# A run-time test moved ahead of the last expert place, and the last layer's x summed in PSUM

## The chip, the cores and the metric

The kernel runs on one core of a Trainium2 chip. The metric is the device time of one execution in microseconds (us); the times below are medians of several executions. The engines are TensorE (PE in the profile, its weight loads PEld), VectorE (DVE), ScalarE (ACT), GpSimd (POOL) and SyncE (SP), which issues most transfers.

## What is computed

Two layers of a trunk work on 256 tokens of x and 256 tokens of a context, each 1024 wide. A layer norms and modulates its input, mixes tokens in three branches (gated linear attention, Fourier, windowed attention), adds the result to x, and then runs a mixture of 16 experts in four groups with two experts for each token. Layer 1, the last, keeps x alone. At the end x is normed once more.

```python
x = x + gate1[:, None, :] * y
h2 = modulate(rms_norm(x, g_ffn), shift2, scale2)
x = x + gate2[:, None, :] * hierarchical_moe(h2, ...)      # out += (silu(h @ w1[e]) * (h @ w3[e])) @ w2[e] * gates[:, e]
...
return rms_norm(x, g_final)                                # after layer 1
```

## The kernel before

The expert stage (`moe`) handles the 16 experts as 16 places, ordered by how many tokens they have. A place is big (B, up to 128 tokens, split in high and low fp32r halves) or small (s, up to 64 tokens, plain fp32). In layer 0 the places are `BBBBsBBsBBsBBsss`, in layer 1 `BBBsssBssssBssss`; the last two are small in both. For a small place PE multiplies the gathered tokens by w1 and w3 (`pair`, L1646, 32 passes in two halves: the first by `begin` in the place before), ACT and DVE make the gated hidden values `th` (L1697, L1658 to L1660), PE transposes them (L1665), and PE multiplies by w2 (L1646, out `c`). The places up to 13 scatter their result rows to a table `yb` in DRAM (L1564). Places 14 and 15 do not: their result is scaled by the gate `gsl`, split in a high and a low half (L1733, L1734), kept in SBUF in a ring slot (`last_y`), and put back to token rows by a product with a one-hot matrix `oh` (`put_rows`, L1776).

Weights come in pieces of 1 MB, each in a ring slot (`wraw`), issued by SP (L245) in the order of `pieces_of` as slots become free. Four slots, `self.spare`, leave the ring before the end. Before the change two of them took the results of places 14 and 15, and two the rows of `yb` (`rows`, L1760), which POOL adds up (L1761); PE then adds them by a product with the identity (L1779) in the same PSUM sum as the one-hot products. DVE multiplies the sum by the modulation `gb` (L1797) and adds it to x (L1799). In layer 0 four row tiles are handled, t = 0 and 1 of x and t = 2 and 3 of the context, which come later; in layer 1 there are two.

If an expert has more tokens than its place can hold, a general path (`moe_general`) adds what is left directly to x. Whether it runs is known only at run time: every engine reads a count `cnti` (L1784, `values_load`) and branches over the block (L1785, `tc.If`). With these inputs the block is not entered. The framework orders instructions by the program's order, the dependences and a planner's estimate of when they are ready; an If is placed as one block. Behind the block, on the path that skips it, each engine waits for its own older work and sets its semaphores as if the block had run; for SP this is its DMA queues. Before the change the block had a pool of its own (`gen`), and stood in the program behind place 15 and the one-hot products of place 14.

At the end (`finish`) ACT squares x from SBUF (L423), POOL takes the power -1/2 (L415), DVE multiplies by the factor and `g_final` (`gf`, L1864), and SP writes 128 rows (L1865). L1912 is the end of the program.

## Time and profile before

| what | us |
|---|---|
| median of 3 runs (lowest, highest) | 1570.74 (1569.88, 1577.3) |
| the profiled execution | 1564.04 |
| its span from the first to the last instruction | 1562.3 |
| mean granted TensorE clock, share of full | 0.975 |

The page lists busy time by engine, the span in slices, the transfers, the chain of work that ended last and the costliest groups of instructions. All times of rows are in us from the start of the span unless marked ns. A row of a timeline merges equal instructions in a stretch; the name before the arrow is what is written, and the brackets hold the idle time of the engine before it and what ended that time. An engine name with q stands for the engine's queue processor: semaphores, branches, register loads and transfer issues.

### The profile page before, as it was taken

How to read it: one execution, taken by the hardware profiler on the slowest of the kernel's cores; microseconds unless marked ns; L12 is line 12 of the kernel's file. 1: busy time of each engine (PE TensorE's matmuls, PEld its weight loads, DVE VectorE, ACT ScalarE, POOL GpSimd, SP SyncE). 2: the span in 40 equal slices, each digit the busy share in tenths (PEclk: the TensorE clock that was granted, in tenths of full speed). 3: DMA queues.
4: the chain of work that ended last, by engine and by line, in shares of the span. 5: the costliest groups of instructions: out<-in, count | busy, mean ns of one | idle time of the engine just before them, and what ended most of it. 6: DMA issues, size and time to landing. Idle time of an engine off the chain costs nothing. (4 is left out here: it accounts for less than half of the span.)

```text
span 1562.3 us, 22623 instructions
## 1 busy us (share of the span) xinstructions
PE 1437.5 (92%) x8333; PEld 1029.9 (66%) x8333; DVE 937.5 (60%) x1757; ACT 746.8 (48%) x1286; POOL 214.0 (14%) x238
## 2 busy tenths in 40 slices
PE   6999899999999998899999979999899979998885
PEld 4666666677777798676665428687689967553521
DVE  4379767432366786897776327467965689341412
ACT  4568556422223232576665306668654448341411
POOL 1124100000111101111111014023001111021001
PEclk9999999999999998999999988999999989999998
DMA  9772242543556578799999863322335699999992
GB/s 325 205 222 92 95 152 68 182 134 122 175 188 203 189 226 317 248 348 379 394 378 385 303 242 118 130 84 82 98 109 185 216 339 334 378 386 394 395 360 120
DMA packets 230795, 363.17 MB, mean 232 GB/s; under 512 B 25676, under 2 KB 125206, under 8 KB 230676
## 3 DMA queue, kind: packets, MB, share of 16 engines
q1 hardware_dynamic: 223808, 349.77, 64.2%
q0 software_dynamic: 6432, 11.76, 2.1%
q8 instruction: 69, 1.13, 0.3%
q14 instruction: 50, 0.41, 0.1%
q10 hardware_dynamic: 436, 0.10, 0.0%
HBM read 350.56 MB, written 21.82 MB: 238 GB/s over the span
## 5 line engine op out<-in xcount | busy, mean ns | idle before, releaser
L266 DVE TENSOR_TENSOR wlo<-wraw,whi 128x1024 fp32r<-128x1024 f32 (+1 forms) x324 | 377.9, 1180 | 184.8 <-ACT whi L265 126.7
L265 ACT ACTIVATE whi<-wraw 128x1024 fp32r<-128x1024 f32 (+1 forms) x324 | 322.3, 1010 | 258.6 <-PE pa L229 110.4
L228 PE MATMUL pa<-hhi,whi 128*128 128x512 f32 (+1 forms) x704 | 240.0, 356 | 1.9 <-ACT qT L795 1.0
L229 PE MATMUL pa<-hlo,whi 128*128 128x512 f32 (+1 forms) x704 | 237.7, 352 | 0.0
L228 PEld LDWEIGHTS pa<-hhi,whi 128*128 128x128 f32 x704 | 133.3, 189 | 27.9 <-issue 10.0
L231 PE MATMUL pa<-hhi,wlo 128*128 128x512 f32 (+1 forms) x704 | 150.5, 349 | 0.0
L1646 PE MATMUL pa<-wraw,xh 128*64 128x512 f32 x520 | 147.2, 626 | 0.0
L229 PEld LDWEIGHTS pa<-hlo,whi 128*128 128x128 f32 x704 | 133.4, 190 | 19.4 <-issue 6.5
L231 PEld LDWEIGHTS pa<-hhi,wlo 128*128 128x128 f32 x704 | 113.5, 190 | 19.2 <-issue 4.8
L1659 DVE SCALAR_TENSOR_TENSOR th<-th,pa 64x512 f32<-64x512 f32 (+1 forms) x32 | 21.7, 679 | 122.6 <-ACT th L1658 122.5
L770 POOL TENSOR_TENSOR m<-m,gu 128x512 f32<-128x512 f32 (+1 forms) x32 | 37.5, 1171 | 403.9 <-DVE gu L768 403.9
L1646 PEld LDWEIGHTS pa<-wraw,xh 128*64 128x64 f32 x520 | 43.7, 142 | 74.4 <-issue 71.3
L235 PE MATMUL pa<-whi,xh 128*128 128x512 f32 x208 | 84.9, 408 | 3.8 <-ACT whi L265 3.7
L236 PE MATMUL pa<-wlo,xh 128*128 128x512 f32 x208 | 85.8, 413 | 1.5 <-DVE wlo L266 1.4
L237 PE MATMUL pa<-whi,xl 128*128 128x512 f32 x208 | 83.6, 402 | 0.1
L1646 PE MATMUL c<-wraw,hh 128*64 128x512 f32 x256 | 69.3, 631 | 1.0 <-DVE hh L1702 1.0
L236 PE MATMUL pa<-y,whi 128*128 128x512 f32 (+1 forms) x192 | 66.3, 345 | 0.9 <-DVE y L272 0.9
L1558 POOL DMA_INDIRECT xg<-h2b,tki x30 | 33.4, 1113 | 242.6 <-PE c L1630 75.1
L235 PE MATMUL pa<-y,whi 128*128 128x512 f32 (+1 forms) x192 | 65.4, 341 | 0.7 <-DVE mx L1150 0.7
L237 PE MATMUL pa<-y,wlo 128*128 128x512 f32 (+1 forms) x192 | 64.9, 338 | 0.0
L359 DVE SCALAR_TENSOR_TENSOR adaw<-adaw,cT 128x512 f32<-128x512 f32 x56 | 45.3, 809 | 25.1 <-DMA adaw<-in_w_ada_dram 24.4
L1564 POOL DMA_INDIRECT yb<-ye,yki x28 | 28.4, 1013 | 220.0 <-ACT ye L1728 111.5
(456 smaller groups left out, 2792.0 us busy)
## 6 DMA issues: line engine op xcount, KB each, us to landing
wraw<-in_w_dram SPq DMA_DIRECT2D x184, 1024.0 KB
wraw<-in_w_in_dram SPq DMA_DIRECT2D x44, 1024.0 KB
adaw<-in_w_ada_dram SPq DMA_DIRECT2D x80, 512.0 KB
adaw<-in_w_ada_dram SPq DMA_DIRECT2D x8, 1024.0 KB
wraw<-in_w_out_dram SPq DMA_DIRECT2D x8, 1024.0 KB
x<-in_w_dram SPq DMA_DIRECT2D x8, 1024.0 KB
yb<-zero SPq DMA_DIRECT2D x12, 512.0 KB
wraw<-yb SPq DMA_DIRECT2D x6, 1024.0 KB
```

The source lines that it names most:

```text
L228: mm(out, lh, rh, start=(i == 0), stop=False)
L229: mm(out, lh, rl, start=False, stop=False)
L231: self.mm = mm(out, ll, rh, start=False, stop=(i == len(ops) - 1))
L235: mm(out, lh, rh, start=start, stop=False)
L236: mm(out, lh, rl, start=False, stop=False)
L237: self.mm = mm(out, ll, rh, start=False, stop=stop)
L265: self.sp = nc.scalar.activation(hv[:, :, q], v[:, :, q], AF.Copy)
L266: self.sl = self.lo.tensor_sub(lv[:, :, q], v[:, :, q], hv[:, :, q].bitcast(F32))
L359: nc.vector.scalar_tensor_tensor(v[:, j], v[:, j], ck, acc, op0=OP.mult, op1=OP.add)
L770: nc.gpsimd.tensor_add(self.m[:, j, :], self.m[:, j, :], u[:, :TY])
L1558: return nc.gpsimd.indirect_dma_start(out=xgs[e % len(xgs)][:n], out_offset=None, in_=h2b, in_offset=bass.IndirectOffsetOnAxis(ap=tki[:n, ...
L1646: nc.tensor.matmul(ps[ts(i, SM)], xs[:, k0[0] + k, :], w[:, k, :], start=(k0[0] + k == 0), stop=(k0[0] + k == k0[1] - 1))
```

## The change

The general path's test is moved from behind place 15 to the start of place 15 (in both layers). Ahead of it all weight pieces that are left are requested in order (`self.got.update(self.pieces)`). The general path has no pool of its own any more: it works in two of the four spare slots (`own`), with smaller weight blocks (512 rows by 128 columns instead of 1024 by 128 or 512 by 256), so it has more and smaller products. The row tiles t = 0 and 1 of `yb` are then loaded in these same two slots.

In layer 1 the results of places 14 and 15 are multiplied by the gate and by the modulation (`gbs`, loaded twice on 64 partitions in place 14) in one DVE operation before they are split. The rows of `yb` are multiplied by `gb` and added to x on DVE, x is added in PSUM by a product with the identity, and then come the one-hot products of place 15. So the new x stands whole in PSUM (`self.last_x`); x in SBUF is not completed. `finish` squares and scales it from PSUM in halves of 512 columns. In layer 0 the sums are made as before, behind the test.

```diff
         for e in range(NE):
+            if e == NE - 1:
+                self.got.update(self.pieces)
+                own = [self.spare.pop(0).tile([P, 2048], F32, name="wraw") for _ in range(2)]
+                n = nc.values_load(cnti[0:1, 0:1], min_val=0, max_val=T)
+                with tc.If(n > 0):
+                    self.moe_general(l, T, h2b, gun, gund, gb, own)
...
                 gb = self.mod_bcast(rp, l, 3, ns, "gb")
+                if l:
+                    gbs = rp.tile([P, 512], F32, name="gbs")
+                    for o in range(2):
+                        nc.sync.dma_start(gbs[ts(o, SM)], self.modd[l][3, 0, ts(o, 512)].partition_broadcast(SM))
...
                 ye = last_y(e)[:, :, :512]
+                if l:
+                    yg = rp.tile([P, 512], F32, name="yg")
+                    V.scalar_tensor_tensor(yg, p2, gsl[:, e:e + 1], gbs, op0=OP.mult, op1=OP.mult)
+                    self.evict_hl(ye[:, 0], ye[:, 1], yg)
+                    continue
...
-            yr = (self.spare.pop(0) if t < 2 else rq).tile([P, 2048], F32, name="wraw").rearrange("p (r d) -> p r d", r=2)
+            yr = own.pop(0) if t < 2 else rq.tile([P, 2048], F32, name="wraw")
+            yr = yr.rearrange("p (r d) -> p r d", r=2)
...
-                if 1 in js:
+                if 1 in js and not l:
                     i = nc.tensor.matmul(pt[o], self.ident, yrs[t][:, 0, ts(o, 512)], start=False, stop=True)
...
-        n = nc.values_load(cnti[0:1, 0:1], min_val=0, max_val=T)
-        with tc.If(n > 0):
-            self.moe_general(l, T, h2b, gun, gund, gb)
+        if l:
+            assert not any(big[NE - 2:])
+            for t in range(nt):
+                yr = yrs[t][:, 0]
+                V.tensor_mul(yr, yr, gb[:, 0])
+                V.tensor_add(self.x[:, t], self.x[:, t], yr)
+                for o in range(2):
+                    nc.tensor.matmul(pts[t][o], self.ident, self.x[:, t, ts(o, 512)], start=False, stop=False)
+            for t in range(nt):
+                put_rows(t, pts[t], (1,))
+            self.last_x = pts
+            sr.close()
+            self.sd.close()
+            return
...
     def finish(self, out):
         for t in range(2):
-            with self.soon(t + 1):
-                r = self.row_rstd(tp, t)
-                o = tp.tile([P, D], F32, name="o", bufs=2)
-                nc.vector.scalar_tensor_tensor(o, self.x[:, t, :], r, gf, op0=OP.mult, op1=OP.mult)
-                nc.sync.dma_start(out[0, ts(t, P), :], o)
+            r = tp.tile([P, 2], F32, name="r", bufs=2)
+            ss = tp.tile([P, 2], F32, name="ss", bufs=2)
+            jk = tp.tile([P, D], BF, name="jk", bufs=2)
+            for h in range(2):
+                nc.scalar.activation(jk[:, ts(h, 512)], self.last_x[t][h], AF.Square, accum_out=ss[:, h:h + 1])
+            nc.vector.tensor_scalar(r[:, 0:1], ss[:, 0:1], 1.0 / D, EPS, op0=OP.mult, op1=OP.add)
+            nc.vector.scalar_tensor_tensor(r[:, 1:2], ss[:, 1:2], 1.0 / D, r[:, 0:1], op0=OP.mult, op1=OP.add)
+            nc.gpsimd.tensor_tensor(r[:, 1:2], r[:, 1:2], self.nhalf[:, 0:1], op=OP.pow)
+            o = tp.tile([P, D], F32, name="o", bufs=2)
+            for h in range(2):
+                nc.vector.scalar_tensor_tensor(o[:, ts(h, 512)], self.last_x[t][h], r[:, 1:2], gf[:, ts(h, 512)],
+                                               op0=OP.mult, op1=OP.mult)
+            nc.sync.dma_start(out[0, ts(t, P), :], o)
```

## Rows read from the trace of the kernel before

**Rows 1.** Page, part 1: busy time, share of the span, instructions of each engine.
```profile
PE 1437.5 (92%) x8333; PEld 1029.9 (66%) x8333; DVE 937.5 (60%) x1757; ACT 746.8 (48%) x1286; POOL 214.0 (14%) x238
```

**Rows 2.** Chain that ended last, in order of time: start, us, what.
```profile
1546.42 3.16 PE pa L1779 x4
...
1553.05 1.44 POOL rsr L415
...
1556.55 1.28 DVE o L1864
```

**Rows 3.** Instructions of line L1785: min/median/max ns, first and last start; below, who waited.
```profile
L1785 SPq EVENT_SEMAPHORE  x16: 17/17/17, 914.8 to 1532.7; - x16
...
L1785 DVEq COMPARE_BRANCH  x2: 63/68/72, 933.3 to 1542.0; - x2
L1785 PEldq COMPARE_BRANCH  x2: 3420/3432/3445, 934.0 to 1542.0; - x2
L1785 DVEq EVENT_SEMAPHORE  x2: 21/21/21, 936.1 to 1542.5; - x2
...
  DVE x L1799: 2.9, 1
```

**Rows 4.** Windows: length, busy (count) of PE, PEld, DVE, ACT, POOL; PE clock, DMA share, GB/s.
```profile
934.40:937.60 3.20, 0.01 (x1) 0.00 (x0) 1.40 (x2) 0.14 (x1) 0.00 (x0) 1.00 0.03 8
937.60:941.20 3.60, 3.50 (x9) 2.30 (x9) 2.14 (x5) 2.16 (x4) 1.39 (x3) 0.54 0.02 5
941.20:946.20 5.00, 3.46 (x16) 3.04 (x16) 2.62 (x1) 1.34 (x3) 5.00 (x3) 0.50 0.00 0
...
1537.00:1541.00 4.00, 3.65 (x16) 1.06 (x16) 0.09 (x1) 0.15 (x1) 0.00 (x0) 1.00 0.00 0
...
1545.60:1549.00 3.40, 3.38 (x6) 1.48 (x6) 0.54 (x1) 0.00 (x0) 0.00 (x0) 0.52 0.02 6
```

**Rows 5.** Timeline, end of layer 1: start, us, engine, line, operation, count, idle before.
```profile
1519.16 0.43 PE L1665 MATMUL c<-ident,th 64*128 64x64 f32 x4 [2.86 <-DVE th L1660]
...
1526.64 0.69 ACT L1733 ACTIVATE wraw<-c,gsl 128x512 fp32r<-128x512 f32 x1 [9.05 <-PE c L1646]
...
1529.70 3.65 PE L1646 MATMUL pa<-wraw,xh 128*64 128x512 f32 x14
...
1540.85 0.69 ACT L1733 ACTIVATE wraw<-c,gsl 128x512 fp32r<-128x512 f32 x1 [6.22 <-PE c L1646]
1541.57 0.75 DVE L1734 SCALAR_TENSOR_TENSOR wraw<-c,gsl,wraw 128x512 fp32r<-128x512 f32 x1 [4.48 <-ACT wraw L1733]
...
1545.62 0.79 PE L1776 MATMUL pa<-wraw,oh 64*128 64x512 f32 x2 [3.30 <-PEq L1785]
...
1554.09 1.06 ACT L423 ACTIVATE jk<-x 128x1024 bf16<-128x1024 f32 x1 [1.35 <-DVE x L1799]
...
1555.05 0.19 ACT L423 ACTIVATION_READ_ACCUMULATOR jk<-x 128x1 f32 x1
...
1555.96 0.56 POOL L415 TENSOR_TENSOR rsr<-rsr,nhalf 128x1 f32<-128x1 f32 x1 [1.46 <-DVE rsr L414]
```

**Rows 6.** Timeline, end of the expert stage of layer 0.
```profile
911.39 0.69 ACT L1733 ACTIVATE wraw<-c,gsl 128x512 fp32r<-128x512 f32 x1 [12.09 <-PE c L1646]
...
913.58 3.65 PE L1646 MATMUL pa<-wraw,xh 128*64 128x512 f32 x14
...
932.63 0.69 DVE L1797 TENSOR_TENSOR wraw<-c,gb 128x512 f32<-128x512 f32 x1 [0.17 <-PE c L1779]
936.21 2.36 DVE L1799 TENSOR_TENSOR x<-x,wraw 128x1024 f32<-128x1024 f32 x2 [2.89 <-DVEq L1785]
```

**Rows 7.** Timeline, the row loads on SP and POOL's additions.
```profile
1519.70 0.88 SPq L1760 DMA_DIRECT2D wraw<-yb  x2
...
1530.47 4.73 POOL L1761 TENSOR_TENSOR wraw<-wraw 128x1024 f32<-128x1024 f32 x2 [15.63 <-DMA wraw<-yb]
```

**Rows 8.** SP's own waits in layer 0, 898 to 925: us in total, times, longest.
```profile
SPq L245 <- DMA wraw<-in_w_in_dram: 4.1, 1, 4.1
```

More of the change, by code (lines that the diff above doesn't have):

```diff
@@ L1666, in hidden @@
             return pt[:, :4 * n]
-        yes = []
+        yes, own = [], []
         def last_y(e):
@@ L1775, in put_rows @@
                             lh, rh = oh[ts(o, SM), j, ts(t, P)], yes[j][ts(o, SM), u, :512]
-                        nc.tensor.matmul(pt[o], lh, rh, start=(j + u == 0), stop=False)
+                        nc.tensor.matmul(pt[o], lh, rh, start=(j + u == 0), stop=(l + j + u == 3))
             for o in range(2):
-                if 1 in js:
+                if 1 in js and not l:
                     i = nc.tensor.matmul(pt[o], self.ident, yrs[t][:, 0, ts(o, 512)], start=False, stop=True)
@@ L1803, in moe, with moe_general @@
         self.dump(f"x2{l}", self.x[:, :nt])
-    def moe_general(self, l, T, h2b, gun, gund, g2):
+    def moe_general(self, l, T, h2b, gun, gund, g2, own):
         nc, io, tc = self.nc, self.io, self.tc
@@ new lines, in moe_general @@
+            h2T = own[0].rearrange("p (k c) -> p k c", k=KD)
+            hr = own[1][:, :D]
+            hid = hr.rearrange("p (f c) -> p f c", f=4)
+            wt = own[1][:, D:D + 512].rearrange("p (k c) -> p k c", k=4)
+            yt, gs = own[1][:, D + 512:D + 640], own[1][:, D + 640:D + 640 + nt]
+            for t in range(2):
+                nc.sync.dma_start(hr, h2b[ts(2 * s + t, P), :])
+                for k in range(KD):
+                    pt = self.c3()
+                    nc.tensor.transpose(pt[:, 0:P], hr[:, ts(k, P)], self.ident)
+                    nc.vector.tensor_copy(h2T[:, k, ts(t, P)], pt[:, 0:P])
@@ new lines, in moe_general @@
+            with tc.For_i(0, NE, 1) as e:
+                nc.sync.dma_start(gs, gund[bass.ds(e, 1)].rearrange("e p t -> p (e t)"))
+                for f in range(4):
+                    ph = []
+                    for w in ("w1", "w3"):
+                        ps = self.c2()
+                        for h in range(2):
+                            nc.sync.dma_start(wt, io[w][l][bass.ds(e, 1), ts(h, 512), ts(f, P)]
+                                              .rearrange("e (k p) c -> p (e k) c", p=P))
+                            for k in range(4):
+                                nc.tensor.matmul(ps[:, :SEQ], wt[:, k, :], h2T[:, 4 * h + k, :], start=(h + k == 0),
+                                                 stop=(h + k == 4))
+                        ph.append(ps)
+                    nc.scalar.activation(hid[:, f, :], ph[0][:, :SEQ], AF.Tanh, scale=0.5)
+                    nc.vector.scalar_tensor_tensor(hid[:, f, :], hid[:, f, :], 1.0, ph[0][:, :SEQ],
+                                                   op0=OP.add, op1=OP.mult)
+                    nc.vector.tensor_mul(hid[:, f, :], hid[:, f, :], ph[1][:, :SEQ])
+                for c in range(KD):
+                    nc.sync.dma_start(wt, io["w2"][l][bass.ds(e, 1), :, ts(c, P)]
+                                      .rearrange("e (k p) c -> p (e k) c", p=P))
+                    for t in range(2):
+                        ps = self.c2()
+                        for f in range(4):
+                            nc.tensor.matmul(ps[:, :P], hid[:, f, ts(t, P)], wt[:, f, :], start=(f == 0), stop=(f == 3))
+                        nc.vector.scalar_tensor_tensor(yt, ps[:, :P], gs[:, 2 * s + t:2 * s + t + 1],
+                                                       g2[:, s, ts(c, P)], op0=OP.mult, op1=OP.mult)
+                        xs = self.x[:, 2 * s + t, ts(c, P)]
+                        nc.vector.tensor_add(xs, xs, yt)
@@ L1860, in finish @@
         for t in range(2):
[L1861 to L1865 removed]
+            r = tp.tile([P, 2], F32, name="r", bufs=2)
[7 more added lines that the diff above has]
+            o = tp.tile([P, D], F32, name="o", bufs=2)
+            for h in range(2):
+                nc.vector.scalar_tensor_tensor(o[:, ts(h, 512)], self.last_x[t][h], r[:, 1:2], gf[:, ts(h, 512)],
+                                               op0=OP.mult, op1=OP.mult)
+            nc.sync.dma_start(out[0, ts(t, P), :], o)
         st.close()
```

41 lines of the change are left out of this document (removed).

## Prediction

> **What bounds the kernel now.** I read the page first. TensorE (PE) is busy for 92% of the span [rows 1], but that share mixes stages, and the change touches only two short ones: the end of the expert stage of layer 0 and the end of layer 1 with the output norm. So I went on to the chain that ended last. It ends with four identity matmuls, the last multiplication `o` and the way out [rows 2]: each step follows the one before it, and the time from the last place's last matmul (1540.8) to the end of the span (1562.3) is 21.5 us of pure latency. Next I looked up the one line that cuts into this chain, the branch of the test (L1785). On PE the branch itself takes 3.42 and 3.45 us, on VectorE (DVE) 0.07 us, but in layer 0 the DVE goes on only at 936.1, 2.8 us after its branch, and the addition to x waits 2.9 us for it [rows 3]. SyncE (SP) shows 16 semaphore steps behind its branch, the last at 1532.7: it takes them only as its own transfers have landed. Last I read the windows behind each branch: PE stands still, and then runs with a granted clock near 0.5, i.e. at 1.2 instead of 2.4 GHz, for 8.6 us in layer 0 and 3.4 us in layer 1 [rows 4].
>
> **Layer 1, the tail.** Before, from the end of w2 of place 15 (the eviction starts at 1540.85) to the end: 21.45 us, in which PE waits 3.30 us for the branch [rows 5], does four products at the low clock [rows 2], and then DVE multiplies and adds, ACT squares 1024 columns, and the norm follows. After the change x is multiplied, added and put into PSUM earlier, so only this is left, counted from the same point:
> - `yg` on DVE: 0.75 us, the duration of L1734, which has the same shape [rows 5]. Then the ACT copy, 0.69 us as L1733 (which reads PSUM; this one reads SBUF), and the subtraction, 0.69 us as a 128x512 DVE operation [rows 6]. With 0.05 us between steps, 2.3 us. Before it was one step less (0.69 + 0.75), so the gate multiplication adds 0.8 us here.
> - PE: the four low products of the two tiles; at 0.26 us (3.65 us for 14 passes of 512 columns [rows 5]) 1.1 us. Tile 0 is whole at 2.9 us, tile 1 at 3.4 us. The high products and the identity products of x lie in PE's wait for `yg`.
> - ACT: four squares of 512 columns. Bounds: half of the 1.06 us square of 1024 columns, or 0.69 us like L1733, since the source is now PSUM; each with 0.19 us for the sum [rows 5]. I take 0.69 + 0.19 (PSUM source); 2.9 + 3.5 = 6.4 us. They run one after another, so ACT and not PE sets tile 1.
> - For tile 1: GpSimd's (POOL) power 0.56 [rows 5], `o` in two halves 2 x 0.69, and an estimated 0.45 for a one-column DVE step and gaps: 2.4 us, so 8.8 us. If POOL takes 1.44 as in its first power [rows 2], 9.7.
> - The way out: `o` ends at 1557.83, the span at 1562.3 [rows 2]: 4.5 us.
> Together 13.3 (to 14.2); I take 13.5, which is **8.0 us less** (7.3 to 8.2). `gf` is needed only by `o`; it can be issued when `gsl` was last read, 0.8 us into this, and there are 5 us for it; I cost it at nothing.
> DVE now also has four operations of 1.2 us (2.36 for two of this size [rows 6]; multiply and add, for two tiles) on `yr`. Those of tile 0 fall into the DVE's idle time ahead of 1540; those of tile 1 can stand ahead of `yg` in its queue. From 0 to 2.4 us, I take **0.7**, because its rows are added by about 1539.8 (below), some 2 us ahead of need.
>
> **Layer 1, the test in place 15.** The If is one block that can't be mixed with other work. Its dependences (PSUM buffers of place 14) are free after w2 of place 14, at 1526.6. There PE took products of place 14 and ended the up-projection of place 15 at 1529.70 + 3.65 = 1533.35, 6.7 us later [rows 5]. With the branch first: 3.43 + 0.1 + 3.65 to 4.1 for the 14 to 16 passes, 0.5 to 0.9 us later than before; the displaced products of place 14 go into the gap of 2.86 us that PE has in each place while DVE makes `th` (1519.16 [rows 5]). To this comes the clock: after both branches of before PE fell to half. A stretch of 3.4 us at half costs 1.7 us; since the ordinary gap of 2.86 us can leave the clock up (1.00 in the w2 of place 15, right behind such a gap [rows 4]), I take 1.0. **1.6 us** in all; bounds 0.4 (branch in the shadow of a gap) and 5.2 (3.5 uncovered and 1.7). Advanced Engine Details and Errata of the Trainium skill, section Control Flow Timing, gives about 108 ns for a compare-and-branch; by it both delays of PE would go and the sum below would be near -10.5 us. The DVE's 0.07 us agrees with the page, PE's 3.42 and 3.45 do not, and the rows decide.
> What queues behind the test: on DVE, ACT and POOL nothing that is due, for DVE's next work is `th`, behind the up-projection. On SP the row loads `wraw<-yb` stand behind it, and they moved from the two last slots into the slots that the If writes, so they wait until PE, DVE and ACT are past the branch (1530.1) and SP's older transfers have landed. Before they were issued at 1519.70 and POOL began to add at 1530.47 [rows 7]. Two loads side by side: the wait of 4.1 us right behind such an issue gives about 5 us for the first [rows 8], and I estimate 6.7 for both. Then POOL's two additions of 2.35 us (9.7), DVE 2.4 (12.1), identity products 2.0 (14.1; 3.16 at the low clock [rows 2]), two squares 1.8, norm and `o` 2.3, way out 4.5: 22.7 us from the branch. 1530.1 + 22.7 = 1552.8, while the other way ends near 1557: hidden by 4 us. The 0.26 MB of `gbs` are small and early.
>
> **Layer 0.** Gone is the stop ahead of x: tile 1's last multiplication ends at 932.63 + 0.69, the additions start at 936.21 [rows 6]. That is 2.9 us; 3.7 if one addition slips between the multiplications. I take **3.2**. In place 15 the same branch: before, the up-projection ended at 913.58 + 3.65 = 917.23, 5.9 us after w2 of place 14 (911.35); with the branch 7.2 to 7.6: 1.3 to 1.7 more, plus clock. I take **2.1**; bounds 0.7 (3.43 + 0.1 less the gap of 2.86) and 7.8 (3.5, and 4.3 for half of 8.6 us at the low clock). The row loads, issued near 915, are added by 925, ahead of the products that end at 932.6. The next layer's first weights stand behind the test on SP as before, where SP's first step behind the branch came only at 914.8 [rows 3]; at nothing.
>
> **The sum.** -8.0 + 0.7 + 1.6 - 3.2 + 2.1 = -6.8 us. The profiled execution took 1564.04 us (span 1562.3 and 1.7 around it), which would become 1557.2. The median of the runs is 1570.74, so I forecast 1564, or 0.43% less. About 0.5% (7.9 us) is what a measurement of this kernel can tell from no change, so the likeliest case lies just inside it; its own range, with each term half way to its bounds (-8.8 to -0.8), is 1562 to 1570.
>
> **Rivals.**
> - A, the clock holds: PE idles behind place 14, but no stretch at half clock follows, and the operations on x find DVE free. For: the clock of 1.00 behind the ordinary gap [rows 4]. Against: both branches of before were followed by half clock. -8.0 + 0 + 0.5 - 3.7 + 1.4 = -9.8, 1561.
> - B, the block falls into the next gap, behind the up-projection (1533.4). Then it costs PE 0.7, but the row loads leave at 1536.9 and end the span at 1559.6: -2.7 in layer 1, -3.2 + 0.7 in layer 0, 1565.5.
> - C, the clock stays low behind the branch for 8.6 us in both places, as in layer 0 before: 4.3 in place of 1.0 and of the 0.6 in the 2.1: -8.0 + 0.7 + 4.9 - 3.2 + 5.8 = +0.2, 1571. TensorE: Matmul & The Clock Gate of the Trainium skill, Part 1, says that "the default state is throttled, and activity releases the throttle"; by that rule the idle branch ahead of the busiest stretch is a poor place for it, and rows 4 agree.
> - D, slower: the block is not moved. The planner may place a block when its last dependence is free, and in layer 0 of before it let four younger multiplications pass it. If it again ends behind place 15, the row loads, now in the If's own slots, start only behind it. Layer 0: PE leaves the branch at 937.4, the rows are added at 947.1 and multiplied at 949.1, x is ready near 951 in place of 938.6: 12.5 late. Layer 1: 1545.6 + 22.7 = 1568.3, 6.0 late. 1589. It decides once PE leaves the branch of layer 1 after 1540 or that of layer 0 after 925. Against: the If's pool of its own, which held it behind place 15, is gone.
>
> **How the numbers follow.** Forecast 0.46, A 0.30, B 0.08, C 0.09, D 0.07. Faster by over 0.5%: most of A (0.27) and the lower end of the forecast (0.13), 0.40. Slower: D and the far end of C, 0.10. The rest, 0.50, within. With all terms at their bounds the sum goes from -10.8 to +5.2; 1558 to 1573 leaves out D and the far end of C, and has 2 us below the best sum for the spread of the runs' median.
>
> **What would show it.** In place 15 of both layers a PE branch of 3.4 us at about 911 and 1527, and none behind place 15; the granted clock of the 4 us after it (0.5 for C, 1.0 for A); DVE's additions in layer 0 directly behind the multiplications; the time from the last w2 matmul to the end of the span, 13.5 us; row loads of layer 1 issued at 1530 and POOL's additions ended by 1540. I am wrong if x in layer 1 comes later than place 15's `yg`, if a weight of place 15 waits, or if ACT's squares from PSUM take much more than 0.69.

## The result, and the profile after

The changed kernel takes 1580.33 us (median of 19 runs) against 1570.74 us for the kernel before (19 runs): ratio 1.0056, 95% interval 1.0036 to 1.0077. It is slower; the forecast was 1564, and the time lies above its range.

The profiled execution of the changed kernel took 1576.29 us (span 1574.5), 12.3 us more than the one of before. The two stretches that the change touches, from the two traces:

| us | before | after | forecast of the change |
|---|---|---|---|
| layer 0, end of w2 of place 14 to end of w2 of place 15 | 14.90 | 19.58 | +2.1 |
| layer 0, from there until x is whole | 12.31 | 8.56 | -3.2 |
| layer 1, end of w2 of place 14 to end of w2 of place 15 | 14.20 | 21.44 | +1.6 |
| layer 1, from there to the end of the span | 21.46 | 23.25 | -8.0 + 0.7 |

First the test. The instructions of its line (min/median/max ns, first and last start) in the kernel after:

```profile
L1681 SPq COMPARE_BRANCH  x2: 53/53/53, 895.7 to 1516.4; - x2
L1681 PEldq COMPARE_BRANCH  x2: 3683/3704/3725, 915.3 to 1540.5; - x2
L1681 DVEq COMPARE_BRANCH  x2: 63/68/72, 915.3 to 1540.5; - x2
```

It did leave the end of the stage [rows 3 have it at 934.0 and 1542.0], but it does not stand right behind place 14, which would have been 907 and 1530. The timeline of layer 1 shows where it fell (start, us, engine, line, operation, count, and in brackets the idle time before it with what ended it):

```profile
1529.86 0.75 DVE L1747 SCALAR_TENSOR_TENSOR yg<-c,gsl,gbs 128x512 f32<-128x512 f32 x1 [9.48 <-PE c L1646]
...
1532.82 5.18 PE L1646 MATMUL pa<-wraw,xh 128*64 128x512 f32 x14
...
1540.04 0.68 DVE L1660 TENSOR_TENSOR th<-th 64x512 f32<-64x512 f32 x1
1540.06 0.50 PE L1794 MATMUL pa<-wraw,oh 64*128 64x512 f32 x1 [2.06 <-DVE th L1659]
1544.34 2.31 SPq L1778 DMA_DIRECT2D wraw<-yb  x2
1544.36 0.76 PE L1794 MATMUL pa<-wraw,oh 64*128 64x512 f32 x1 [3.80 <-PEq L1681]
1544.51 0.66 PE L1665 MATMUL c<-ident,th 64*128 64x64 f32 x4
...
1545.68 5.58 PE L1646 MATMUL c<-wraw,hh 128*64 128x512 f32 x16 [0.52 <-DVE hh L1709]
1549.92 2.34 POOL L1779 TENSOR_TENSOR wraw<-wraw 128x1024 f32<-128x1024 f32 x1 [34.97 <-DMA wraw<-yb]
1551.32 0.75 DVE L1747 SCALAR_TENSOR_TENSOR yg<-c,gsl,gbs 128x512 f32<-128x512 f32 x1 [5.68 <-PE c L1646]
...
1555.31 2.71 PE L1809 MATMUL pa<-x,ident 128*128 128x512 f32 x4 [4.05 <-DVE x L1807]
...
1564.30 0.60 ACT L1891 ACTIVATE jk<-pa 128x512 bf16<-128x512 f32 x1 [11.57 <-PE pa L1794]
```

The reader should see three things. PE's branch stands between the gate's VectorE steps and the transposes: one product of place 14 (1540.06), which the gate's first VectorE step (L1659, writing `th`) released, is ahead of it, so the branch begins when the gap is nearly over, and all of its 3.8 us delays the transposes (1544.51, which could have started at 1540.8). The row loads are issued at 1544.34, the moment PE is past the branch. And the products of x with the identity come after place 15's `yg`, not ahead of it: until the first square 13 us pass behind w2 (1551.3 to 1564.3), where 2.9 were forecast. The chain that ended last says the same (start, us, what); 9.04 us of it is the second row load:

```profile
1544.90 9.04 DMA wraw<-yb
...
1554.15 3.31 POOL wraw L1779
...
1560.03 3.57 PE c L1809 x4
```

### The profile page after: what moved, and what is told of

Its sections match the earlier page's. It is cut to its first block, busy times and chain, and to the rows that moved or that the text cites. A ratio compares the mean times of both kernels' runs of the same rounds, so it can differ in the third digit from the quotient of the medians.

```text
span 1574.5 us, 22631 instructions
## 1 busy us (share of the span) xinstructions
PE 1442.6 (92%) x8333; PEld 1032.8 (66%) x8333; DVE 938.4 (60%) x1761; ACT 747.0 (47%) x1290; POOL 218.4 (14%) x238
## 5 line engine op out<-in xcount | busy, mean ns | idle before, releaser
L1659 DVE SCALAR_TENSOR_TENSOR th<-th,pa 64x512 f32<-64x512 f32 (+1 forms) x32 | 21.7, 680 | 123.4 <-ACT th L1658 110.4
```

## The experiments

Each row's ratio is to the kernel before, run beside it, with its 95% interval. "Layer 0" is the time from the end of place 14's w2 products to the first product with the next layer's weights, "place 15" and "tail" are layer 1's two stretches as in the table above, all from one profiled execution each; "PE at the branch" is the length of TensorE's branch record in layer 0 and layer 1. That is not always idle time, since products queued ahead of the branch can still run while it lasts: in layer 1 of e3, e4, e7 and e10 the branch held TensorE idle for 2.3, 0, 0.7 and 0 us, in the other entries of 3 us or more for 3.1 to 6.7 us.

| run | ratio | layer 0 | place 15 | tail | PE at the branch |
|---|---|---|---|---|---|
| before | 1 | 38.99 | 14.20 | 21.46 | 3.4, 3.4 |
| e11 before again | 1.0005 (0.9978 to 1.0032) | 40.56 | 17.18 | 22.47 | 3.7, 4.1 |
| after | 1.0056 (1.0036 to 1.0077) | 40.21 | 21.44 | 23.25 | 3.7, 3.7 |
| e1 after, no test | 0.9952 (0.9928 to 0.9975) | 40.24 | 20.79 | 21.07 | none |
| e5 before, no test | 0.9905 (0.9878 to 0.9931) | 35.22 | 15.91 | 16.58 | none |
| e2 own rows | 1.0012 (0.9988 to 1.0036) | 38.76 | 21.24 | 19.07 | 3.9, 3.3 |
| e3 no drain | 1.0029 (1.0008 to 1.0051) | 45.48 | 16.26 | 19.02 | 6.7, 7.0 |
| e4 path on GpSimd's queue | 1.0013 (0.9992 to 1.0033) | 43.04 | 15.77 | 21.01 | 3.8, 3.9 |
| e8 layer 0 as before | 1.0039 (1.0018 to 1.0060) | 40.51 | 21.25 | 21.91 | 3.6, 3.3 |
| e6 sums first, no test | 0.9928 (0.9909 to 0.9947) | 38.12 | 21.66 | 12.99 | none |
| e9 sums between, no test | 0.9901 (0.9868 to 0.9934) | 38.36 | 17.24 | 14.55 | none |
| e7 own rows, sums first | 0.9998 (0.9976 to 1.0019) | 43.18 | 15.42 | 13.17 | 3.9, 6.6 |
| e10 test in the gap | 1.0029 (1.0005 to 1.0053) | 38.95 | 17.75 | 14.59 | 3.6, 3.9 |
| e12 before, short body | 0.9940 (0.9911 to 0.9970) | 38.36 | 17.16 | 16.99 | 0.4, 0.2 |
| e13 before, path in loops | 0.9970 (0.9942 to 0.9997) | 39.06 | 17.18 | 17.76 | 3.3, 0.3 |
| e16 before, shorter still | 0.9962 (0.9935 to 0.9989) | 39.13 | 17.19 | 16.86 | 0.35, 0.34 |
| e14 after, path in loops | 1.0016 (0.9993 to 1.0039) | 40.22 | 20.93 | 22.05 | 3.3, 0.4 |
| e15 all together | 0.9976 (0.9956 to 0.9997) | 37.49 | 26.06 | 14.60 | 3.4, 0.3 |
| e17 all mended | 0.9941 (0.9918 to 0.9965) | 40.43 | 12.01 | 15.21 | 0.35, 0.34 |

Three theories went in. T1: the loss is the row loads, which wait for the branch because the If writes their slots. T2: it is TensorE's branch and the half clock around it. T3: the tail from PSUM is longer than worked out, since the row sums are queued behind place 15's eviction.

### The test, its place and the rows (e1 to e4, e8)

**e1** leaves the If out of the changed kernel.

```diff
-                n = nc.values_load(cnti[0:1, 0:1], min_val=0, max_val=T)
-                with tc.If(n > 0):
-                    self.moe_general(l, T, h2b, gun, gund, gb, own)
```

> The changed kernel without the general path and its test (with these inputs it is never entered); everything else stays. Theory 1: the changed kernel is slow because its row loads, in slots that the If writes, wait until PE has left the branch, which fell into place 15. Theory 2: the branch costs PE itself 3.7 us in each layer and the low clock behind it, and the row loads do not matter. Theory 3: the new tail from PSUM is longer than I worked out. By 1 and 2 there is nothing left to wait for: the row loads leave near 1520, the time from the last w2 product to the end of the span is 13 to 15 us, and the time is about 1560 (some 10 under the kernel before, ratio 0.992 to 0.995). By 3 that tail stays above 18 us and the time is within 3 us of the kernel before.

The ratio fell as T1 and T2 wanted, but the tail did not follow: 21.07 us with no test at all. Its timeline shows why. POOL had summed the rows at 1531, yet VectorE's queue has `yg` first:

```profile
1540.81 6.22 PE L1646 MATMUL c<-wraw,hh 128*64 128x512 f32 x16 [0.52 <-DVE hh L1706]
...
1547.08 0.75 DVE L1744 SCALAR_TENSOR_TENSOR yg<-c,gsl,gbs 128x512 f32<-128x512 f32 x1 [6.33 <-PE c L1646]
1547.75 1.22 DVE L1803 TENSOR_TENSOR wraw<-wraw,gb 128x1024 f32<-128x1024 f32 x1
...
1550.76 3.78 PE L1806 MATMUL pa<-x,ident 128*128 128x512 f32 x4 [3.73 <-DVE x L1804]
```

So T3 holds beside the others, by order and not by the size of its steps. Place 15 did not get shorter either (20.79 us), though no test stands in it: its up-projection and its w2 products took 6.24 and 6.22 us at a mean granted clock of 0.58, against 3.65 us each at 1.00 in the profile of before. So the length of place 15 in a single profile does not give the price of a test.

**e2** gives layer 1's rows slots that the If doesn't touch.

```diff
+                rw = self.pool(sr, "rows3", bufs=2, side="right") if l else None
...
-            yr = own.pop(0) if t < 2 else rq.tile([P, 2048], F32, name="wraw")
+            yr = (rw if l else own.pop(0) if t < 2 else rq)
+            yr = yr.tile([P, 2048], F32, name="wraw") if l or t >= 2 else yr
```

> The changed kernel with the two row tiles of layer 1 in slots of their own, which the If does not write; the test stays in place. Theory 1: the row loads wait only for SP's older transfers (near 1527) and are added by about 1540, so the end follows w2 of place 15 by 13 to 15 us instead of 23: 8 to 9 us under the changed kernel, ratio to the kernel before 0.999 to 1.002. Theory 2: place 15 still ends 10 us late, and the time stays within 3 us of the changed kernel, ratio 1.004 to 1.007.

The rows left at 1531.9, 12.7 us ahead of PE's branch, and the tail lost 4.2 us, which is 0.27% of the time:

```profile
1531.87 0.93 SPq L1780 DMA_DIRECT2D wraw<-yb  x2
```

By the medians T1 is worth 0.44% of the 0.56%; from the two intervals I estimate an uncertainty of 0.3% to either side, so T1 is a real part of the loss, of a size known only roughly. Place 15 stayed at 21.2 us.

**e3** drops the line that puts the last four weight loads ahead of the test on SyncE; **e4** drops it too and puts the general path's transfers on GpSimd's queue.

```diff
-                self.got.update(self.pieces)
...
-        nc.sync.dma_start(hr, h2b[ts(2 * s + t, P), :])
+        nc.gpsimd.dma_start(hr, h2b[ts(2 * s + t, P), :])
...
```

> The changed kernel without the line that requests all weights of place 15 ahead of the test. In the instruction order the branch then stands right behind the eviction of place 14, where I forecast it, but the four weights of place 15 stand behind SP's test and its wait for older transfers. Theory 1: the row loads leave near 1531 and are ready in time; if the weights come in time too, 8 to 12 us under the changed kernel (1568 to 1572); if the weights are late (issued from about 1522, 5 us for the first, some 2.7 for each further), place 15 starts 3 to 5 us later and the time is about 1573. Theory 2: PE pays the branch in front of the up-projection instead of behind it, and the time stays within 3 us of the changed kernel.

> As without the request line, and the general path's own transfers are issued by POOL instead of SP, so SP has no transfers in the block and does not wait for landings behind its branch. Theory 1: the place-15 weights are issued without a stop and the row loads leave when PE is past the branch, near 1531: the forecast of the prediction, about 1562 to 1565, ratio 0.994 to 0.997. Theory 2: PE's branch of 3.4 us and the low clock in place 15 of both layers keep it at 1572 or above, ratio 1.001 or more.

In both the test stands where it was forecast: TensorE's branch begins at 1528.3 and 1532.1 in layer 1, as place 14's w2 products start to run, and place 15 is back at 16 us. Those products were queued ahead of the branch and cover most of it. Of its 7.05 us in e3 TensorE is idle for 2.34; in e4 it ends (1536.0) before the products do (1536.1) and costs TensorE nothing.

```profile
1535.50 0.47 PE L1793 MATMUL pa<-wraw,oh 64*128 64x512 f32 x1 [2.34 <-PEq L1680]
```

So the drain is what had pushed the block one gap further (how the planner reckons that is argued, not shown). But layer 0 lost most of what layer 1 won (45.5 and 43.0 us). There the branch is uncovered (TensorE is idle for 6.70 us in e3 and 3.10 in e4), the up-projection and w2 behind it run partly at half clock (5.36 and 4.94 us in e3, 5.09 and 6.33 in e4), and the gate's second step takes 2.51 and 2.72 us beside POOL's addition. The forecast place is better than the one taken by 0.43% in e4 and by 0.27% in e3, the latter within the noise, and still no gain over the kernel before.

**e8** puts layer 0's test back behind the one-hot products, with tiles of its own.

```diff
-            if e == NE - 1:
+            if l and e == NE - 1:
```

> The changed kernel with layer 0's last place, test and general path as before (the test behind the one-hot products, tiles of its own); layer 1 as changed. From the two profiles layer 0's change is a wash: its end loses 3.7 us (additions follow multiplications directly) and its place 15 gains 4.6 us, so taking it back is worth 0.9 us: ratio 1.004 to 1.006, and the whole loss is layer 1's. Rival: the loss sits in layer 0's longer place 15 (3 us or more): ratio 1.003 or less. Rival: layer 0's gain stood and layer 1 lost more than the median shows: ratio 1.0075 or more.

At 1.0039 it lies at the lower edge: layer 0 has 0.17 of the 0.56%, with intervals as wide as that, and layer 1 the rest.

### What a test costs (e5, e12, e13, e16, e14, e11)

**e5** is the kernel before without its test.

```diff
-        n = nc.values_load(cnti[0:1, 0:1], min_val=0, max_val=T)
-        with tc.If(n > 0):
-            self.moe_general(l, T, h2b, gun, gund, gb)
```

> The kernel before without the general path and its test (left out in both layers); all else as before. Theory T2 (a test costs what TensorE stands at its branch): 3.4 us in layer 0 and 3.3 us in layer 1 of the profile before, of which layer 1's eviction of place 15 (2.3 us) would have stood there anyway: 4 to 6 us less, ratio 0.996 to 0.998. Theory T1 as far as it applies here (the cost of the test after is the place in the order where it was put, since row loads, weight loads and sums are fenced behind it): before, the row loads are ahead of the test and nothing but the sums stands behind it, so the test costs before at most what it costs TensorE, ratio 0.995 to 1.000, against the 16 us (1.0 per cent) that it costs in the changed kernel. If the ratio here is 0.990 or less, the test costs as much in the one kernel as in the other and T1 falls.

0.95%, against 1.04% in the changed kernel (1.0056 less 0.9952): the two tests cost some 15 us in either, so moving them saved nothing. That is at the edge of the 0.990 at which its expectation gives T1 up; T1 is a part of the loss (e2) and not the whole. And without tests the changed kernel is slower than the old one (0.9952 against 0.9905): most of what separates the two kernels is there without any test. In the two profiles that difference lies in all three stretches: 5.0 us in layer 0 (for its cause see e9), 4.9 in place 15 (most of it the clock, see e1) and 4.5 in the tail. It doesn't add to e2's 0.44%; the sums are late twice over, since the rows are late and since their place in the queue is behind `yg`, and mending one of the two uncovers the other.

**e12** keeps the test and puts four short instructions behind it in place of the general path.

```diff
-        for s in range(T // SEQ):
-            ...
+        nc.tensor.transpose(pt[:, 0:P], self.x[:, 0, 0:P], self.ident)
+        nc.vector.tensor_copy(self.x[:, 0, 0:P], pt[:, 0:P])
+        nc.scalar.activation(self.x[:, 0, P:2 * P], pt[:, 0:P], AF.Copy)
```

> The kernel before, its test kept in both layers, but behind it instead of the general path one transposition on TensorE, one copy on VectorE, one on ScalarE and one transfer (the general path's work is left out; it is not taken for these inputs). H1 (the price of the test is the jump over a long body, on TensorE some 180 instructions): TensorE stands under 0.5 us at the branch and the ratio is 0.991 to 0.994, most of what e5 without any test showed (0.9905). H2 (the price is the branch itself and the fence that it is for the order of the work): 3.3 to 3.4 us at the branch as before and 0.998 to 1.000. H3 (branch short, but the fence costs): under 0.5 us and 0.996 to 0.998.

H1 (the price is the jump over a long body) holds for TensorE, and the ratio lies in H1's range. TensorE now spends 0.22 and 0.36 us on what took 3.4 (same test, same place, not taken):

```profile
L1785 PEldq COMPARE_BRANCH  x2: 219/288/358, 934.7 to 1544.9; - x2
```

**e13** keeps all the work but writes the path as loops; **e16** loops over the token halves too; **e14** is e13's edit in the changed kernel.

```diff
-                    for f in range(4):
+                    with tc.For_i(0, 4, 1) as f:
...
-        for s in range(T // SEQ):
+        with tc.For_i(0, T // SEQ, 1) as s:
```

> The kernel before, the general path's products, transposes and transfers written as loops (over k, f and c) in place of unrolled, so that TensorE jumps over some 120 instructions in layer 0 and 60 in layer 1 in place of some 360 and 180; all of it computes what it did. H1 (the price of a test that is not taken is the length of the jump): TensorE stands 0.2 to 0.5 us at the branch, as in e12_short_body, and the ratio is 0.993 to 0.996. H4 (any body longer than the few instructions of e12 costs the same step): 3.3 us or more at the branch and 0.998 to 1.001.

> The kernel before, its general path as loops as in e13 and a loop over the two halves of the tokens too, so that TensorE's body has some 60 instructions in layer 0 as well; all of it computes what it did. In e13 TensorE stood 3.3 us at layer 0's branch (some 120 instructions) and 0.3 us at layer 1's (60). H1 (a longer jump costs, and in steps): 0.2 to 0.5 us at both branches, ratio 0.993 to 0.996. H4 (what counts is where the code falls, not the length): 3.3 us at one or both, on TensorE or on another engine, and 0.996 to 1.000.

> The changed kernel with its general path as loops, nothing else. H1: TensorE's 3.7 us at each of the two branches become 0.2 to 0.5 us, some 6.6 us less than the changed kernel's 1.0056: ratio 1.000 to 1.002; the rest of its loss (rows behind the branch, sums behind the last eviction) stays. H4: 1.004 to 1.007.

The same line in e13, then in e16:

```profile
L1785 PEldq COMPARE_BRANCH  x2: 344/1846/3349, 933.4 to 1550.3; - x2
```

```profile
L1785 PEldq COMPARE_BRANCH  x2: 335/344/352, 939.2 to 1556.2; - x2
```

Counted from the instruction lists, TensorE jumps over 239 (layer 0) and 120 (layer 1) in the kernel before, 303 and 152 after, 123 and 62 in e13, 69 and 69 in e16 (the expectations name other counts, made by eye). A branch record over 120 and more lasts 3.3 to 7.0 us in every run, over 69 and fewer 0.2 to 0.4: on TensorE a step, not a slope. Length is not all of it, since the same body of the changed kernel takes 3.3 to 3.9 us in after, e2 and e4 and 6.6 to 7.0 in e3 and e7. The Trainium skill, Runtime: NRT & Kernel Launch, section Instruction fetch mechanics, says that a taken branch whose target lies outside the window already fetched has to wait for the fetch. TensorE's step agrees with such a wait and shows its price; that a fetch is what it waits for, no run here shows.

The ratios follow H1 only in part: e14's 1.0016 lies in its range, e13's 0.9970 and e16's 0.9962 lie above theirs. Layer 0 shows a reason. There the additions to x wait for VectorE, which goes on some 3 us after its own branch in before, e13 and e16 alike, so the 3 us that e16 takes off TensorE's branch bring nothing there (39.13 us, against 38.99 and 40.56 in the two profiles of before). Of the kernels with a test only e12, with its very short body, lets VectorE go on after 0.6 us in layer 0. In e16:

```profile
941.57 2.36 DVE L1799 TENSOR_TENSOR x<-x,wraw 128x1024 f32<-128x1024 f32 x2 [3.06 <-DVEq L1785]
```

On VectorE the length of the body does not sort the cases: e16's body is the same in both layers, and VectorE goes on 2.9 us after the branch in layer 0 and 0.5 us after it in layer 1; in layer 1 of e13 and e14 it takes 3.0 and 2.8 us, where before and after took 0.5 and 0.2. So H4, that what counts is where the code falls, stays open beside H1, and which engine pays changes with small edits.

**e11** is the kernel before itself.

> The kernel before itself, for a second profile and as a control: ratio 0.998 to 1.002. The theory on the clock (the profile of before fell on an execution whose last 70 us held almost no stretch at half clock, so it stands some 6 us under the median, and the tails of the two profiles differ by more than the kernels do): the stretch from the end of place 14's w2 products in layer 1 to the end, 35.7 us there, measures 37 to 42 us here. Rival: 35 to 36.5 us again, and the profiles compare as they stand.

The control is 1.0005, but its profile took 1574.11 us against the first one's 1564.04. One window (length, busy time of PE, PEld, DVE, ACT, POOL, granted clock of PE, DMA share, GB/s) and the w2 products of place 15, first from the first profile and then from the second:

```profile
1520.00:1530.00 10.00, 9.22 (x40) 2.98 (x38) 0.80 (x2) 0.69 (x1) 0.00 (x0) 1.00 1.03 415
...
1537.15 3.65 PE L1646 MATMUL c<-wraw,hh 128*64 128x512 f32 x16 [0.52 <-DVE hh L1702]
```

```profile
1520.00:1530.00 10.00, 7.88 (x26) 2.70 (x28) 1.79 (x3) 0.54 (x1) 0.00 (x0) 0.66 1.03 416
...
1543.44 6.41 PE L1646 MATMUL c<-wraw,hh 128*64 128x512 f32 x16 [0.52 <-DVE hh L1702]
```

It is the same kernel, once at full clock and once with more than half of the window at 1.2 GHz: the same products take 3.65 us in the one and 6.41 in the other, and place 15 14.20 and 17.18. Against this profile the change costs 4.3 us in place 15, 0.8 in the tail and nothing in layer 0, some 5 us of the 8.8 by which the medians differ. So how the loss divides between the stretches is known only as far as e1, e2 and e8 show it.

### The order of the sums (e6, e9)

Both leave the test out, as e1 does. **e6** queues VectorE's four operations on the rows ahead of place 15's gate and the identity and place 14's one-hot products ahead of its transposes; **e9** queues the four between the copy of the transposed rows and `yg`.

```diff
+            if l and e == NE - 1:
+                early()     # e6: rows, sums and products ahead of place 15
...
+                    self.behind(m, i)         # e9: the first sum behind hh's copy
...
+                        self.behind(i, sums[0])   # and yg behind the last sum
```

> The changed kernel without the general path and its test (left out), as in e1_no_test_after, and with the row sums' multiplication and addition into x queued on VectorE ahead of place 15's gate, and the identity products and the one-hot products of place 14 queued on TensorE ahead of place 15's transposes. Theory T3 (the tail is long because these four VectorE operations and twelve products are queued behind place 15's eviction): the stretch from the end of place 15's w2 products to the end of the kernel falls from 21.1 us to 13.5 to 15 us, the forecast's figure; against e1's 0.9952 the ratio falls to 0.990 to 0.992. Rival T4 (the work does not vanish: the same 5 to 6 us of VectorE and 3 to 6 us of TensorE only lengthen place 15 instead, or the rows arrive too late for it): the tail gets shorter and place 15 longer by as much, ratio 0.994 to 0.997, no different from e1.

> The changed kernel without the general path and its test (left out), the row sums' multiplications and additions into x queued on VectorE between place 15's copy of the transposed rows and its yg, so under TensorE's w2 products of place 15; TensorE's order as in the changed kernel. T3 (the length of the new tail is its order on VectorE): the four operations of 1.22 us each fit under the 5.6 us of w2 products, so place 15 stays at the 15.9 us of e5_before_no_test and the stretch behind it falls to 14 to 15 us; from the end of place 14's w2 products to the end of the kernel 30 to 31 us, against 41.9 us in e1, 34.7 in e6 and 32.5 in e5; ratio 0.988 to 0.991. T4 (the sums cannot be hidden in place 15 wherever they stand): 34 to 36 us and 0.992 to 0.995.

e6's tail is 12.99 us: the forecast's steps were right (13.5). But its ratio lies above T3's range, and place 15 is 5.75 us longer than e5's: the gate waits for the sums, and the first multiplication takes 3.35 us while POOL still adds.

```profile
1528.56 3.35 DVE L1714 TENSOR_TENSOR wraw<-wraw,gb 128x1024 f32<-128x1024 f32 x1 [2.23 <-POOL wraw L1688]
```

In e9 the same four fit under the w2 products, at 1.22 us each, and PE goes from w2 straight to the identity products:

```profile
1535.21 1.21 DVE L1721 TENSOR_TENSOR wraw<-wraw,gb 128x1024 f32<-128x1024 f32 x1
1535.35 3.65 PE L1646 MATMUL c<-wraw,hh 128*64 128x512 f32 x16 [0.52 <-DVE hh L1717]
...
1538.85 1.22 DVE L1723 TENSOR_TENSOR x<-x,wraw 128x1024 f32<-128x1024 f32 x1
1538.93 1.98 PE L1815 MATMUL pa<-x,ident 128*128 128x512 f32 x4
1539.99 0.74 DVE L1762 SCALAR_TENSOR_TENSOR yg<-c,gsl,gbs 128x512 f32<-128x512 f32 x1
```

e1's 0.9952 became 0.9901 (the two intervals just overlap), from the order of VectorE's queue: the row loads leave at about the same point, 10.0 us ahead of the end of place 14's w2 products in e1 and 8.4 in e9. T3 holds as a matter of order; T4 (the sums can't be hidden) falls.

e9 only equals e5 (0.9905), though its place 15 and tail together are 0.7 us shorter: its layer 0 is 3.1 us longer. There too the order on VectorE shows. The norm of x's first tile (`xr`, which waits for POOL) stands ahead of the second tile's multiplications, where in e5 they follow the first addition at once. So x's two tiles are whole 11.3 us behind w2 of place 15, in e1 as well, against 8.5 us in e5:

```profile
924.32 0.75 DVE L532 TENSOR_SCALAR xr<-x,rsr 128x1024 f32<-128x1024 f32 x1 [0.76 <-POOL rsr L415]
...
924.99 1.28 DVE L1832 TENSOR_TENSOR wraw<-c,gb 128x512 f32<-128x512 f32 x2
```

In e1 one more piece shows. POOL's second row addition runs beside the gate, whose second step takes 2.60 us in place of 0.68:

```profile
907.43 2.35 POOL L1776 TENSOR_TENSOR wraw<-wraw 128x1024 f32<-128x1024 f32 x1 [2.81 <-issue]
907.73 2.60 DVE L1660 TENSOR_TENSOR th<-th 64x512 f32<-64x512 f32 x1
```

### Put together (e7, e10, e15, e17)

All four compute everything. **e7** is e4 with e2's slots and e6's order (products behind place 15's up-projection).

> The whole computation: the test right behind place 14 (no drain of the planner's weight loads, the general path's transfers on GpSimd's queue, as in e4_pool_dma), layer 1's rows in slots of their own and loaded ahead of the test, and the sums and products queued ahead of place 15's gate and transposes as in e6_sums_first. T3 and T1 together: against e4's 1.0013 the tail loses 6 to 7.5 us, ratio 0.996 to 0.998. T4: 1.000 to 1.003.

A miss: its ratio lies above the forecast range. The tail is 13.17 us as in e6, but layer 0 has e4's 43 us. Layer 1's branch, though 6.55 us long, is not what it lost: place 14's products cover all but 0.66 us of it.

**e10** has layer 0 as before, layer 1's test behind place 14's up-projection, and e9's order.

```diff
+                if l and e == NE - 2:
...
+                    for ld in lds:            # the loads of the count; PE's stands behind m14
+                        g_ = {mybir.EngineType.PE: m14, mybir.EngineType.DVE: g14[1], mybir.EngineType.Activation: g14[0]}.get(ld.ins.engine)
```

> The whole computation. Layer 0's last place, test and general path as before; layer 1's test in place 14's gap, where TensorE has issued its products and waits for the gate (4 to 5 us in the profile of the changed kernel), the general path in slots that nothing else uses, the rows loaded ahead of place 15, the sums as in e9_sums_between. If a test costs what TensorE stands at its branch beyond its other waits: 0 to 1 us in layer 1 in place of 3.3 us, and with e9's order about 2 us less behind place 15: ratio 0.996 to 0.998. Rival (half of what e5 showed for two tests, 7 us, is paid wherever the test stands): ratio 0.999 to 1.002.

A miss by its own fault: a row load stands ahead of the test on SyncE and waited until 1519.4 for place 13's scatter, SyncE then needed 5.0 us from its branch to the next step, and the next weights left only at 1525.7:

```profile
1525.66 2.51 SPq L245 DMA_DIRECT2D wraw<-in_w_dram  x4
```

PE had 1.9 us of work between 1523.3 and 1533.8. TensorE's own branch, 3.90 us from 1514.6, lies wholly beside products of place 14 that run until 1519.1. What the gap hides of a whole test was not measured.

**e15** takes e13's loops, layer 0 as before, layer 1's test right behind place 14 with slots of its own, weights and then rows behind it, and e9's order.

> The whole computation: the general path as loops in both layers; layer 0's last place and test as in the kernel before; layer 1's test right behind place 14 with slots of its own, the weights of place 15 and then the rows loaded behind it, the sums between place 15's copy and yg as in e9_sums_between. From the parts: e13's ratio (0.994) less 2 to 4 us for layer 1's new tail in e9's order against e5's: 0.990 to 0.993. Rival (the new tail brings nothing even in its best order, e9's 0.9901 against e5's 0.9905): 0.994 to 0.996, no better than e13. Rival (the test in front of place 15 delays its weights or rows): 0.997 or more.

A miss: 0.9976 is its last rival's case. The tail is e9's (14.60), but VectorE stood 5.27 us behind its own branch with place 14's subtraction, and PE's products and the up-projection stood behind that:

```profile
1533.47 2.44 DVE L272 TENSOR_TENSOR wraw<-yg,wraw 128x512 fp32r<-128x512 f32 x1 [5.27 <-DVEq L1693]
```

**e17** moves that subtraction ahead of the test and place 14's one-hot products behind the up-projection, with e16's path.

```diff
+                    if ld.ins.engine == mybir.EngineType.DVE:
+                        self.behind(ld, lo14)
...
+                            self.behind(i, m15)
```

> The whole computation, as e15_all_together, with e16's path in both layers, place 14's subtraction on VectorE ahead of the test, and place 14's one-hot products on TensorE behind place 15's up-projection, so that nothing of TensorE waits for VectorE's branch (5.3 us in e15) until the gate of place 15. Forecast from e15: place 15 falls from 26.1 to 17 to 18 us, the stretch from the end of place 14's w2 products to the end from 40.7 to 32 us, ratio 0.990 to 0.994, better than both kernels. Rival (another engine's branch takes its place): 0.995 or more.

0.9941 (0.9918 to 0.9965), 1561.58 us, at the edge of its range and with a shorter place 15 (12.01 us) than expected: with all the work, ahead of both kernels. Against e16, the old kernel with the same loops, it gains 0.2%, which the intervals don't tell from nothing. The up-projection follows w2 of place 14 at once, and VectorE's stand behind its branch (3.69 us) lies beside it, but for the last 0.8 us, for which the gate waits:

```profile
1531.77 3.65 PE L1646 MATMUL pa<-wraw,xh 128*64 128x512 f32 x16
...
1537.48 0.68 DVE L1660 SCALAR_TENSOR_TENSOR th<-th,pa 64x512 f32<-64x512 f32 x1 [3.69 <-DVEq L1697]
```

## Why the prediction was wrong

Set against the forecast, the profile of after is 9.1 us too long in layer 1's tail, 5.6 in its place 15 and 2.6 in layer 0's place 15.

**Layer 1's tail, -8.0: the steps right, one premise wrong.** `yg` 0.75, ACT's copy 0.63 (forecast 0.69), the subtraction 0.69, squares from PSUM 0.60 + 0.20 (0.69 + 0.19), the power 0.56: in e6 they gave 12.99 us, in e17 15.21. The step that failed is "The high products and the identity products of x lie in PE's wait for `yg`", with its price of 0.7 (bound 0 to 2.4) for VectorE's four operations. The planner queued them behind `yg` in layer 1 of after as in e1, where the rows had been ready for 15 us. The operations, then eight identity products partly at half clock, then the one-hot products came one after the other: 21.07 us without a test, 6.5 more than in e9's order and 8.1 more than in e6's, in place of 0.7. I had read that VectorE is idle and not where its queue would put the work. Half of the -8.0 was also no gain of the tail: the old tail without its test is 16.58 us (e5), 4.9 less than with it, so the new tail is worth 2.0 us (e9) to 3.6 us (e6, which pays for it in place 15); the rest was the price of the test, which went elsewhere.

**The test in place 15, +1.6 (bounds 0.4 to 5.2): the place was wrong.** It fell into the next gap, which was rival B with a chance of 0.08. B priced PE's share at 0.7, as if the branch would start when the up-projection ended; a product that waits for `th` stands ahead of it, so 3.8 us were added. Place 15 grew by 7.2 us between the two profiles, by 4.3 against e11; 3.5 of the 7.2 is the clock (up-projection and w2 took 5.18 and 5.58 us in place of 3.65 each). The cause of the place is the drained loads ahead of the test on SyncE (e3), which the prediction left out. In the forecast place the branch costs TensorE 2.3 us (e3) or nothing (e4) in layer 1, less than the 3.43 us that the prediction set ahead of the up-projection, since place 14's queued w2 products cover it; in layer 0 it stays uncovered. That place would have been better by 0.43% (e4; e3's 0.27% is within the noise), not by enough for a gain.

**The rows, "hidden by 4 us".** They left at 1544.3, where B had 1536.9, and the end followed 30.2 us after PE was past the branch, in place of 22.7: the first load 5.6 us (forecast 5), the second 9.6 (6.7), identity products at half clock, the one-hot products again behind them. That is T1: 0.44% (e2), give or take 0.3%. Rival D's rule for deciding, PE past layer 1's branch after 1540, was met though the block had moved.

**Layer 0, -3.2 and +2.1.** The additions follow the multiplications: -3.75 us. Place 15 got 4.7 us longer (3.6 against e11), of which the branch itself is 3.7; the +2.1 had put part of it under the gap. The sum is near zero, as e8's 0.17% shows.

**The clock.** The 1.0 us behind each branch can't be told apart: the stretches at 1.2 GHz lie at other places in each execution. The profile of before that carried all the terms had none between 1480 and 1540; the clock of 1.00 in [rows 4] came from there, and I took it for the rule; the gap right ahead of that stretch was 2.05 us and not the 2.86 of place 14. That profile lay 6.7 us under the median.

**The price of a branch.** The Trainium skill, Advanced Engine Details and Errata, section Control Flow Timing, gives about 108 ns for a compare-and-branch; the rows of before showed 3.4 us [rows 3] and I let them decide. TensorE's branch is above the page's figure in every run: 0.22 to 0.36 us over a short body, 3.3 to 7.0 over a long one. VectorE's compare alone took 0.06 to 0.07 us, but its next step came 0.2 to 5.6 us later.

What stays open: the medians of e5 and e12 differ by 0.35%, with intervals that overlap, so whether a test with a short body costs nothing isn't settled; nor is why VectorE needs 3.7 to 5.3 us behind a body of 57 instructions in e15 and e17, why TensorE's branch doubles in e3 and e7, or whether the new tail, with everything mended, gains on the old kernel with the same loops.

## What to carry to other kernels

An operation is hidden only where its engine's queue has it ahead of what the end waits for: when work moves off a tail, fix its place in the queue (here four operations between one copy and one eviction, 0.5% from e1 to e9). On TensorE the price of a test that isn't taken was a jump over a long body, so write the rare path as loops before looking for a better place for the test; then look at every other engine that has code in the body, since here VectorE's 3 us in layer 0 stayed. A branch behind a long run of queued products is covered by them (e4, e10). And compare two profiles only after a second one of the same kernel: here it moved one stage by 3 us of 14.

## What the runs showed of the hardware

- TensorE's branch record lasts 3.3 to 7.0 us over 120 or more listed instructions and 0.2 to 0.4 over 69 or fewer, with the test not taken in either. Products queued ahead of it run on meanwhile: 3.86 us of branch in e4 and 3.90 in e10 left TensorE no idle time, 6.55 in e7 left 0.66.
- VectorE's compare takes 0.06 to 0.07 us, but its next step came 2.9 us later in layer 0 of e16 and 0.5 us later in layer 1, over the same body.
- GpSimd's addition of two SBUF tiles slows a two-input SBUF operation on VectorE beside it: 1.22 to 3.35 us (e6), 0.68 to 2.60 (e1). The Trainium skill, Trainium Architecture — The Big Picture, section What this means for kernel authors, calls the port that the two share an exclusive lock. The rows agree: in both VectorE ends 0.6 to 1.1 us behind POOL's addition, about its own time alone.
- The granted clock of the same kernel in the same 10 us was 1.00 in one execution and 0.66 in another (e11).
